# Scaling the halves of the up product ahead of the silu, exchanging two carried products, reordering a leftover pair and pinning row additions in a two-layer trunk

## The chip, the cores and the metric

The kernel runs on one core of one Trainium2 chip. The metric is the device time of one execution in microseconds; the smaller the better. The kernel before took 1260.61 us, the median of 3 runs (1259.55 to 1261.18).

## What is computed

The reference is a trunk of two layers of a hybrid decoder: a residual mixer (attention heads beside retention heads) and a residual SwiGLU feed-forward network (FFN), on 16 learned tokens and 512 given ones, with 1024 features. The change touches the FFN alone:

```python
D_MODEL = 1024; SEQ = 512; DEPTH = 2; N_META = 16
D_FF = -(-8 * D_MODEL // (3 * 256)) * 256        # 2816
...
    mix = jnp.concatenate([fox_out, ret_out], axis=-1)
    h = h + jnp.einsum('blc,cd->bld', mix, w_out)

    hn = rmsnorm(h, ffn_norm_g)
    ff = jax.nn.silu(jnp.einsum('bld,df->blf', hn, w_gate)) * jnp.einsum('bld,df->blf', hn, w_up)
    return h + jnp.einsum('blf,fd->bld', ff, w_down)
...
    h = rmsnorm(h, final_norm)
    return h[:, N_META:]
```

## The kernel before

**Data.** The state h lies transposed in SBUF, eight tiles of 128 features by 528 tokens. Layer 0 works on all 528 columns, the FFN of layer 1 on the 512 that are returned. Each fp32 factor is split into a high part hi, a rounded copy that ScalarE (ACT) makes by a cast, and a low part lo, the rest, that VectorE (DVE) subtracts. A product is the three matmuls hi·xh, hi·xl, lo·xh on TensorE (PE), for each block of 128 of the contraction.

**The FFN in units.** The 2816 hidden features are 22 blocks of 128 (`NF`). Blocks 0 to 2 are done plainly, blocks 3 to 21 by the class `Unit`, one object for each block. A unit computes gate and up of its block together by seven products instead of eight, on half columns (w = 264 in layer 0, 256 in layer 1) and half of the contraction (`HB` = 4 blocks, so 12 matmuls each); `p(i)` gives product i, in the order 1, 2, 6, 5, 7, 4, 3. Products 1, 6, 7 and 4 accumulate into the bank x (pool psa, four buffers of one bank), 2 goes into z, 5 and 3 into y (pool psd, two buffers of two banks). After products 1, 6 and 7 `keep` (L960) copies the bank x on ACT into e (L965), and product 4 then ends x. After product 3, `done` (L971) makes the activation: sg = zy + e (L975), times RSC·R (L977, R is the row's normalisation), silu on ACT (L978, which is the helper's line L407; behind the last block's silu a helper loads the next table of ACT, L409), u = sg·(−RSC)·R (L980), the first half of u times x (L982), the second times e[2] (L983); then u is split into ab and xh (L142 the cast, L143 the subtraction), for every second block after sums of parts (L992, L999 to L1001).

**The FFN's second matrix in pairs.** The hidden blocks are worked off in rounds of four (`ROUNDS`). After a round, the class `Down` multiplies it into h, two output blocks (a pair, p = 0 to 3) at a time, again by seven products, of two blocks (6 matmuls) each. Products 1, 6, 7, 4 go into a psa bank x, 2 into z, 5 and 3 into y of a psd buffer. `keep` (L1078) copies x, and y after product 5, on ACT into S (L1084); so product 4, which adds to x, waits for the copy after product 7, and product 3, which adds to y, for the copy after product 5. `done` (L1099), after product 3, adds z and y to S on DVE (L1102) and so releases the psd buffer. `add` (L1091) adds S to the two rows of h: by an accumulating DMA on POOL's queue, or, for the leftover pair, on DVE (L1097).

**Order.** The lists in the planning loop (L1177 to L1232) interleave the pairs of one round with the units of the next. PE runs in the order of these lists (L1512); the instructions of the other engines are put into an order by a scheduler, unless `pin` (L307) keeps one in the order of the program. Four pairs meet four units, but in the last round only three (blocks 19, 20, 21): the fourth pair, the leftover pair e, follows beside block 21 (L1203). For p = 0 the list (L1191) ends with (d, 7); the two products that are left, 4 and 3, the hang, are carried into the next unit, behind its product 1 (L1201, L1205). Eight such hangs are in the program, four in each layer.

**The last round** (blocks 19 to 21) goes into h plainly: `down_job` (L1115) loads and splits its weights by `splits` (L885: the cast L886, the subtraction L887), `down` (L1132) multiplies (L1148) and adds to h (L1163). In layer 1 the products of this round are planned apart (L1240 on): eight products of the first 272 columns, with row sums on DVE from psa (`add_part`, L1249), then eight of the other 240, among them the final normalisation and the output.

Weights of units: `make1` to `make4`, by `splits` or by ACT (L938) and DVE (L939, L940); weights of pairs: `make_a`, `make_b` (L1058 to L1065), with sums that POOL makes ahead of them (L1050 to L1056).

Of the kernel before, what the change touches and what calls it, by code (L numbers as in the profile page):

```python
# [10 lines left out]
F32 = mybir.dt.float32  # L11
F32R = mybir.dt.float32r
AF = mybir.ActivationFunctionType
ALU = mybir.AluOpType
# [11 lines left out]
NF = DFF // 128  # L26
# [13 lines left out]
def hybrid_kernel(ctx, tc, x_t, w_in, w_fl, w_out, w_gate, w_up, w_down, vecs, b_fg, rope, decay, mask, ident, out_t):  # L40
    nc = tc.nc
# [9 lines left out]
    h = [state.tile([128, T], F32, name=f"h{k}") for k in range(NK)]  # L51
# [89 lines left out]
    def split(hi, lo, src, pinned=False):  # L141
        pin(nc.scalar.copy(hi, src), pinned)  # L142
        pin(nc.vector.tensor_sub(lo, src, hi.bitcast(F32)), pinned)  # L143
# [122 lines left out]
    def tt(name, dt=F32):  # L266
        tag, bufs = tags[name]
        return tmp.tile([128, T], dt, name=name, tag=tag, bufs=bufs)
# [4 lines left out]
    def fft(tag, dt=F32R, shape=(128, T), bufs=None):  # L273
        return phase["ffn"].tile(list(shape), dt, name=tag, tag=tag, bufs=bufs)
# [28 lines left out]
    RSC = -1.0 / (2.0 * D)  # L303
# [3 lines left out]
    def pin(f, pinned=True):  # L307
        if pinned:
            tc.keep_in_program_order(f)
# [96 lines left out]
    def silu(t, then=None):  # L406
        nc.scalar.activation(t, t, AF.Silu)  # L407
        if then:
            tc.keep_in_program_order(nc.scalar.preload_act_table_set(then))  # L409
# [384 lines left out]
    def ffn(l, st, real, last):  # L794
        QC = REAL if real else FULL
        t0 = META if real else 0
        w = (T - t0) // 2
# [5 lines left out]
        def two(t):  # L803
            return t[:, t0:T].rearrange("p (a b) -> p a b", a=2)
# [6 lines left out]
        def act_tile(f):  # L811
            t = buf(0).rearrange("p i s c -> p (i s c)")
            i = f if f < PLAIN else f - ROUNDS[-1][0]
            return [t[:, (2 * i + j) * T:(2 * i + j + 1) * T] for j in range(2)]
# [60 lines left out]
        def add_job(**job):  # L875
            job["ring"] = "f" if len(jobs) % 2 else ""
            jobs.append(job)
            return len(jobs) - 1
# [3 lines left out]
                if i <= j or "make" in jobs[i]:  # L882
                    convert(i)

        def splits(hi, lo, src):  # L885
            nc.scalar.copy(hi, src)  # L886
            nc.vector.tensor_sub(lo, src, hi.bitcast(F32))  # L887

        def product(j, o, x, bank, fresh, final, n=HB, done=None):

# [14 lines left out]
        class Unit:  # L905
# [65 lines left out]
            def done(self):  # L971
                e = self.t["e"]
                sg = tt("sg")
                with tc.high_priority():
                    nc.vector.tensor_add(two(sg), self.t["zy"][:, :, 0:w], e[:, 0:2])  # L975
                c = slice(t0, T)
                nc.vector.scalar_tensor_tensor(sg[:, c], sg[:, c], RSC, st["R"][:, c], ALU.mult, ALU.mult)  # L977
                silu(sg[:, c], None if self.f < NF - 1 else ROOTS if last else LOGS)  # L978
                u = tt("tq")
                nc.vector.scalar_tensor_tensor(u[:, c], sg[:, c], -RSC, st["R"][:, c], ALU.mult, ALU.mult)  # L980
                u2 = two(u)
                nc.vector.tensor_mul(u2[:, 0], self.t["x"][:, 0:w], u2[:, 0])  # L982
                nc.vector.tensor_mul(u2[:, 1], e[:, 2], u2[:, 1])  # L983
                if self.f >= ROUNDS[-1][0]:
                    fh, fl = act_tile(self.f)
                    split(fh[:, c], fl[:, c], u[:, c])
                    acts[self.f] = (fh, fl)
                    return
                q, second = divmod(self.f - PLAIN, 2)
                if not second:  # L990
                    us[q] = u2, two(tt("tq"))
                    nc.vector.tensor_sub(us[q][1][:, 0], u2[:, 1], u2[:, 0])  # L992
                    return
                u0, ta = us.pop(q)
                tb = two(tt("tq"))
                parts = [(0, 1, u0[:, 0:1]), (1, 2, u2), (3, 2, ta), (5, 2, tb)]
                for i, (s, n, src) in enumerate(parts):
                    if i == 2:
                        nc.vector.tensor_sub(tb[:, 0], u2[:, 1], ta[:, 0])  # L999
                        nc.vector.tensor_sub(tb[:, 1], u2[:, 1], u0[:, 1])  # L1000
                        nc.vector.tensor_sub(ta[:, 1], u2[:, 0], tb[:, 0])  # L1001
                    ph, pl = slots(q, s, n, 0), slots(q, s, n, 1)
                    m = n // len(ph)
                    for j in range(len(ph)):
                        split(ph[j], pl[j], src[:, j * m:(j + 1) * m])
# [27 lines left out]
        class Down:  # L1033
# [57 lines left out]
            def add(self, s):  # L1091
                m = 2 * self.m + s
                e = self.t["e"][:, 2 * s:2 * s + 2]
                if self.dma:
                    adds.append(lambda: nc.gpsimd.dma_start(two(h[m]), e, accum_op=ALU.add))  # L1095
                else:
                    nc.vector.tensor_add(two(h[m]), e, two(h[m]))  # L1097

            def done(self):  # L1099
                e = self.t["e"][:, 0:2]  # L1100
# [14 lines left out]
        def down_job(p, f0, f1, own=False):  # L1115

            n = f1 - f0
            t = {}

            def load():  # L1120
                if t:
                    return
                if own:
                    t["r"] = fft("fraw", F32, (128, NK, 128), 2)
                else:
                    t["r"] = wp.tile([128, NK, 128], F32, name="raw", tag="raw", bufs=3)
                for s in range(2):
                    nc.sync.dma_start(t["r"][:, s * n:s * n + n], w_down[l, 2 * p + s, :, f0:f1])

            return add_job(load=load, make=lambda hi, lo: splits(hi, lo, t["r"][:, 0:2 * n]), n=2 * n)  # L1130

        def down(j, s, m, f0, f1, banks, far=False):  # L1132

# [42 lines left out]
        hang = []  # L1176
        for r, (f0, f1) in enumerate(ROUNDS):  # L1177
            for f in range(f0, f1):
                if f < PLAIN:
                    steps += dense_steps(w_gate[l, f], [(0, xs, NK, QC, g_done(f) if f else held.append)], banks=f == 1)  # L1180
                    steps += dense_steps(w_up[l, f], [(0, xs, NK, QC, u_done(f))])
                    continue
                u = Unit(f, r > 1)
                if r > 1 and fills:
                    p = fills.pop(0)[0]
                    if p == 0:
                        u.rest()
                        d = Down(p, r - 1, True)
                        u.last()
                        d.second()  # L1190
                        order = ((u, 1), (u, 2), (u, 6), (u, 5), (u, 7), (d, 1), (d, 2), (u, 4), (d, 6), (d, 5), (u, 3), (d, 7))  # L1191
                    else:
                        d = Down(p, r - 1, True)
                        u.rest()
                        d.second()
                        if f == NF - 1:
                            e = Down(fills.pop(0)[0], r - 1, False)
                        u.last()
                        if f == NF - 1:
                            e.second()  # L1200
                        order = [(u, 1)] + hang + [(u, 2), (d, 1), (u, 6), (d, 2), (u, 5), (d, 6), (u, 7), (d, 5), (d, 7),  # L1201
                                                   (u, 4), (d, 4), (d, 3), (u, 3)]
                        if f == NF - 1:  # L1203
                            order[-1:] = [(e, 1), (u, 3)] + [(e, i) for i in (2, 6, 5, 7, 3, 4)]
                    hang = [(d, 4), (d, 3)] if p == 0 else []  # L1205
                    for o, i in order:
                        steps += o.p(i)
                        if o is u and i == 6 or o is not u and f == NF - 1 and i == 4:
                            steps.append(flush)
                    continue  # L1210
                steps += u.head()
                for v in tails:
                    v.last()
                    steps += v.tail()
                tails = []
                u.rest()
                steps += u.middle()
                if fills:
                    p, g0, g1 = fills.pop(0)
                    j = down_job(p, g0, g1)  # L1220
                    steps += down(j, 0, 2 * p, g0, g1, not real, r < len(ROUNDS) - 1)
                    u.last()
                    steps += u.tail()
                    steps += down(j, 1, 2 * p + 1, g0, g1, False, r < len(ROUNDS) - 1)
                else:
                    tails = [u]
            for p, g0, g1 in fills:
                j = down_job(p, g0, g1)
                for s in range(2):
                    steps += down(j, s, 2 * p + s, g0, g1, False)  # L1230
            assert not fills or r < 2
            fills = [(p, f0, f1) for p in range(NK // 2)]  # L1232
        n = f1 - f0
# [355 lines left out]
```

## Time and profile before

| | |
|---|---|
| median of 3 runs | 1260.61 us (1259.55 to 1261.18) |
| the profiled execution | 1260.84 us, its span 1259.1 us |
| granted TensorE clock, mean | 0.998 |
| PE busy | 1239.7 us (98%), 9463 matmuls |
| weight loads (PEld) busy | 1194.2 us (95%) |
| DVE busy | 1036.9 us (82%), 1980 instructions |
| ACT busy | 782.9 us (62%), 1572 instructions |
| POOL busy | 558.8 us (44%) |

The profile is of one execution, with times from the start of the span. A row of the timeline has the start, the duration, the engine, the line, the operation, the tile that is written and those that are read, their shapes, and in brackets how long the engine was idle just before and what released it. Two instructions of an engine overlap at their ends, so what one costs its engine is read from start to start. A row of the waits says which instruction waited for which, with the sum, the number of times and the longest. A row of the grouped instructions has the count, the busy time in us and the mean in ns. The row of a window has the stretch and its length, then busy us (and instructions) of PE, PEld, DVE, ACT and POOL, the granted clock, the DMA engines' share and GB/s.

### The profile page before, as it was taken

Reading aid. Unit: us, or ns where it says so; the run is one execution under the profiler, and the core shown is the slowest. Engines: PE = TensorE matmul, PEld = TensorE weight load, DVE = VectorE, ACT = ScalarE, POOL = GpSimd, SP = SyncE. Lnnn points to the kernel's source line nnn. Section 1 sums busy time; section 2 is a strip of 40 time slices with the busy share of each in tenths; the row PEclk is TensorE's granted clock in tenths of the full one; section 3 lists DMA queues with packets and bytes.
Section 4 is the critical chain, followed back from the end, with each engine's and each line's share of the span. In section 5 each row is a group of like instructions: output and inputs, shape, how many; then the busy total and the mean of one; then the engine's idle time right before and its main releaser. Section 6 shows DMA issues by size and latency. Waiting matters only on the chain. (4 is left out here: it accounts for less than half of the span.)

```text
span 1259.1 us, 25291 instructions
## 1 busy us (share of the span) xinstructions
PE 1239.7 (98%) x9463; PEld 1194.2 (95%) x9463; DVE 1036.9 (82%) x1980; ACT 782.9 (62%) x1572; POOL 558.8 (44%) x866
## 2 busy tenths in 40 slices
PE   9999999999999999999999999999999999999996
PEld 8999999999999999999999989999789999999996
DVE  7877855779778999899886877567897899999987
ACT  6666545676556666666666665557765566666665
POOL 3355546421135555554325545454112545655440
PEclk9999999999999999999999999999999999999999
DMA  6322232226687878786423222222367877878751
GB/s 219 94 69 85 77 87 82 62 83 181 157 193 160 205 168 209 171 200 148 123 78 119 69 97 80 79 91 68 127 159 187 196 184 186 186 183 189 173 135 67
DMA packets 73051, 170.80 MB, mean 136 GB/s; under 512 B 8400, under 2 KB 15312, under 8 KB 72928
## 3 DMA queue, kind: packets, MB, share of 16 engines
q1 hardware_dynamic: 50576, 128.70, 31.7%
q0 software_dynamic: 21888, 40.17, 19.9%
q8 instruction: 74, 1.21, 0.4%
q14 instruction: 49, 0.40, 0.1%
q10 hardware_dynamic: 464, 0.32, 0.1%
HBM read 146.79 MB, written 2.13 MB: 118 GB/s over the span
## 5 line engine op out<-in xcount | busy, mean ns | idle before, releaser
L194 POOL TENSOR_TENSOR wlo<-raw,whi 128x128 fp32r<-128x128 f32 x504 | 258.6, 548 | 280.4 <-ACT whi L191 280.3
L217 PE MATMUL psd<-xh,whi 128*128 128x264 f32 (+1 forms) x792 | 196.3, 315 | 0.5 <-ACT whi L191 0.5
L217 PE MATMUL psd<-xh,wlo 128*128 128x264 f32 (+1 forms) x792 | 187.0, 304 | 0.0
L217 PE MATMUL psd<-xl,whi 128*128 128x264 f32 (+1 forms) x792 | 186.6, 303 | 0.4 <-DVE xl L320 0.4
L217 PEld LDWEIGHTS psd<-xh,whi 128*128 128x128 f32 x792 | 128.8, 190 | 5.5 <-ACT whi L191 1.2
L217 PEld LDWEIGHTS psd<-xh,wlo 128*128 128x128 f32 x792 | 127.4, 189 | 6.3 <-DVE wlo L194 0.4
L217 PEld LDWEIGHTS psd<-xl,whi 128*128 128x128 f32 x792 | 128.0, 189 | 4.7 <-DVE xl L320 0.8
L191 ACT CAST whi<-raw 128x512 fp32r<-128x512 f32 (+1 forms) x168 | 98.5, 613 | 51.9 <-PE psd L217 36.9
L926 POOL DMA_DIRECT2D Sw<-w_up x38 | 34.0, 911 | 168.1 <-DMA Sw<-w_up 38.0
L1095 POOL DMA_DIRECT2D h<-S x60 | 54.3, 914 | 84.4 <-ACT S L1084 33.1
L887 DVE TENSOR_TENSOR wlo<-raw,whi 128x1024 fp32r<-128x1024 f32 (+1 forms) x62 | 76.7, 1248 | 16.5 <-ACT whi L886 16.3
L886 ACT CAST whi<-raw 128x1024 fp32r<-128x1024 f32 (+1 forms) x62 | 58.8, 954 | 40.4 <-issue 10.3
L898 PE MATMUL psa<-th,fwhi 128*128 128x264 f32 (+1 forms) x256 | 72.5, 283 | 0.0
L898 PE MATMUL psa<-tl,fwhi 128*128 128x264 f32 (+1 forms) x256 | 72.5, 283 | 0.0
L898 PE MATMUL psa<-th,fwlo 128*128 128x264 f32 (+1 forms) x256 | 72.4, 283 | 0.0
L927 POOL DMA_DIRECT2D fraw<-w_gate x38 | 33.4, 880 | 85.4 <-DVE xl L320 40.4
L965 ACT COPY e<-psa 128x264 f32<-128x264 f32 (+1 forms) x114 | 42.6, 374 | 37.3 <-PE psa L898 37.0
L527 ACT ACTIVATE probs<-probs,nmax 128x144 f32<-128x144 f32 (+1 forms) x64 | 36.9, 576 | 44.4 <-DVE nmax L514 31.5
L898 PE MATMUL psa<-ab,fwhi 128*128 128x264 f32 (+3 forms) x304 | 59.7, 285 | 0.7 <-ACT S L1084 0.6
L898 PE MATMUL psa<-th,whi 128*128 128x264 f32 (+1 forms) x200 | 56.8, 284 | 0.2
L898 PE MATMUL psa<-th,wlo 128*128 128x264 f32 (+1 forms) x200 | 56.1, 281 | 0.0
L898 PE MATMUL psa<-tl,whi 128*128 128x264 f32 (+1 forms) x200 | 56.1, 281 | 0.0
(370 smaller groups left out, 4468.5 us busy)
## 6 DMA issues: line engine op xcount, KB each, us to landing
raw<-w_in SPq DMA_DIRECT2D x54, 512.0 KB, 3.5
raw<-w_gate SPq DMA_DIRECT2D x44, 512.0 KB, 4.9
fraw<-w_up SPq DMA_DIRECT2D x38, 512.0 KB, 5.8
raw<-w_down SPq DMA_DIRECT2D x64, 256.0 KB, 4.3
h<-S POOLq DMA_DIRECT2D x38, 264.0 KB, 5.3
Sw<-w_up SPq DMA_DIRECT2D x38, 256.0 KB, 3.9
fraw<-w_gate POOLq DMA_DIRECT2D x38, 256.0 KB, 4.1
Sw<-w_up POOLq DMA_DIRECT2D x38, 256.0 KB, 6.6
```

Source lines behind the costliest of these rows:

```text
L191: pin(nc.scalar.copy(hi, job["raw"][:, c0:c1]), pinned)
L194: pin(sub(lo[:, i:i + step], job["raw"][:, c0 + i:c0 + i + step], hi[:, i:i + step].bitcast(F32)), pinned)
L217: nc.tensor.matmul(ps[1][b][:, 0:c1 - c0], w[:, wk, :], x[:, c0:c1], start=(k == 0 and i == 0), stop=(k == n - 1 and i == 2))
L527: nc.scalar.activation(pr, pr, AF.Exp, bias=nmax[0:nq], scale=-1.0, accum_out=rsum)
L886: nc.scalar.copy(hi, src)
L887: nc.vector.tensor_sub(lo, src, hi.bitcast(F32))
L898: nc.tensor.matmul(bank()[:, 0:b.shape[-1]], a[:, o + k, :], b, start=(fresh and k == 0 and i == 0), stop=(k == n - 1 and i == 2), skip_gr ...
L926: nc.gpsimd.dma_start(s, w_up[l, self.f][:, 0:HB], accum_op=ALU.add)
L927: nc.gpsimd.dma_start(self.t["b"][:, 0:HB], w_gate[l, self.f][:, 0:HB], accum_op=ALU.add)
L965: nc.scalar.copy(self.t["e"][:, i], self.t["x"][:, 0:w])
L1095: adds.append(lambda: nc.gpsimd.dma_start(two(h[m]), e, accum_op=ALU.add))
```

## The change

Five edits:

1. `splits` gets an argument `pinned`; the subtraction of the last round's weights, for the pairs p = 2 and 3, is kept in program order.
2. In `Unit.done`, x and e[2] are scaled by −RSC·R into the two halves of u ahead of the silu (two scalar_tensor_tensor of a half each). Behind the silu stands one product u = sg·u over all columns, in place of a whole scalar_tensor_tensor and two products of a half.
3. In `Down.add`, the addition of rows on DVE (the leftover pair alone) is kept in program order.
4. The leftover pair's products go in the order 1, 5, 6, 2, 7, 3, 4 instead of 1, 2, 6, 5, 7, 3, 4.
5. The hang is product 3, then 4, instead of 4, then 3. Each is followed by its own row addition, so the two accumulating DMAs are issued in the other order too.

```diff
-        def splits(hi, lo, src):
+        def splits(hi, lo, src, pinned=False):
             nc.scalar.copy(hi, src)
-            nc.vector.tensor_sub(lo, src, hi.bitcast(F32))
+            pin(nc.vector.tensor_sub(lo, src, hi.bitcast(F32)), pinned)
...
                 nc.vector.scalar_tensor_tensor(sg[:, c], sg[:, c], RSC, st["R"][:, c], ALU.mult, ALU.mult)
+                u = tt("tq")
+                u2, r2 = two(u), two(st["R"])
+                for i, v in enumerate((self.t["x"][:, 0:w], e[:, 2])):
+                    nc.vector.scalar_tensor_tensor(u2[:, i], v, -RSC, r2[:, i], ALU.mult, ALU.mult)
                 silu(sg[:, c], None if self.f < NF - 1 else ROOTS if last else LOGS)
-                u = tt("tq")
-                nc.vector.scalar_tensor_tensor(u[:, c], sg[:, c], -RSC, st["R"][:, c], ALU.mult, ALU.mult)
-                u2 = two(u)
-                nc.vector.tensor_mul(u2[:, 0], self.t["x"][:, 0:w], u2[:, 0])
-                nc.vector.tensor_mul(u2[:, 1], e[:, 2], u2[:, 1])
+                nc.vector.tensor_mul(u[:, c], sg[:, c], u[:, c])
...
-                    nc.vector.tensor_add(two(h[m]), e, two(h[m]))
+                    pin(nc.vector.tensor_add(two(h[m]), e, two(h[m])))
...
-            return add_job(load=load, make=lambda hi, lo: splits(hi, lo, t["r"][:, 0:2 * n]), n=2 * n)
+            return add_job(load=load, make=lambda hi, lo: splits(hi, lo, t["r"][:, 0:2 * n], f1 == NF and p > 1), n=2 * n)
...
-                            order[-1:] = [(e, 1), (u, 3)] + [(e, i) for i in (2, 6, 5, 7, 3, 4)]
-                    hang = [(d, 4), (d, 3)] if p == 0 else []
+                            order[-1:] = [(e, 1), (u, 3)] + [(e, i) for i in (5, 6, 2, 7, 3, 4)]
+                    hang = [(d, 3), (d, 4)] if p == 0 else []
```

In the changed kernel the scaled halves are line 981 and the product is line 983.

The scheduler makes another order of it on ACT and DVE too. On PE, the third hang of layer 0, a piece of the difference; psd is the buffer of product 3, psa with xh of 4144 that of product 4, ab the operand slots of the round:

```order
 L898 MATMUL psa<-xl_4153,whi 128x264
 L898 MATMUL psa<-xh_4152,wlo 128x264
+L898 MATMUL psd<-ab_4348,fwhi 128x264 x2
+L898 MATMUL psd<-ab_4348,fwlo 128x264
+L898 MATMUL psd<-ab_4346,fwhi 128x264 x2
+L898 MATMUL psd<-ab_4346,fwlo 128x264
 L898 MATMUL psa<-xh_4144,fwhi 128x264
 L898 MATMUL psa<-xl_4145,fwhi 128x264
```

Product 3 stands directly behind the unit's product 1 (its last rows are the two without a sign); product 4 follows.

On ACT, the end of the leftover pair and of block 21 in layer 1, before (S is the pair's sum tile, sg and tq belong to block 21's activation, fwhi and fraw to the last round's weights):

```order
L1084 COPY S<-psa 128x256
L886 CAST fwhi<-fraw 128x768
L1084 COPY S<-psd 128x256
L1084 COPY S<-psa 128x256
L407 ACTIVATE sg<-sg 128x512
L409 ACT_TABLE_LOAD
L1084 COPY S<-psa 128x256
L886 CAST fwhi<-raw 128x768
L142 CAST ab_12249<-tq 128x512
```

The same place after:

```order
L1084 COPY S<-psd 128x256
L1084 COPY S<-psa 128x256
L407 ACTIVATE sg<-sg 128x512
L886 CAST fwhi<-fraw 128x768
L1084 COPY S<-psa 128x256
L409 ACT_TABLE_LOAD
L1084 COPY S<-psa 128x256
L142 CAST ab_12249<-tq 128x512
L886 CAST fwhi<-raw 128x768
```

The copy of psd (product 5) and the silu moved ahead of the cast of fraw, and the cast of ab ahead of that of raw.

On DVE, the same stretch, before:

```order
L975 TENSOR_TENSOR sg<-psd,e 128x512
L887 TENSOR_TENSOR wlo<-fraw,whi 128x768
L977 SCALAR_TENSOR_TENSOR sg<-sg,R 128x512
L887 TENSOR_TENSOR fwlo<-fraw,fwhi 128x768
L1086 TENSOR_TENSOR S<-S 128x256
L1102 TENSOR_TENSOR S<-psd,S 128x512
L980 SCALAR_TENSOR_TENSOR tq<-sg,R 128x512
L1097 TENSOR_TENSOR h_79<-S,h_79 128x512
L982 TENSOR_TENSOR tq<-psa,tq 128x256
L983 TENSOR_TENSOR tq<-e,tq 128x256
L1097 TENSOR_TENSOR h_80<-S,h_80 128x512
L887 TENSOR_TENSOR fwlo<-raw,fwhi 128x768
```

After, up to the first row sum of the last round:

```order
L977 SCALAR_TENSOR_TENSOR sg<-sg,R 128x512
L983 TENSOR_TENSOR tq<-sg,tq 128x512
L887 TENSOR_TENSOR fwlo<-fraw,fwhi 128x768
L1102 TENSOR_TENSOR S<-psd,S 128x512
L1086 TENSOR_TENSOR S<-S 128x256
L1097 TENSOR_TENSOR h_79<-S,h_79 128x512
L143 TENSOR_TENSOR ab_12249<-tq,ab_12249 128x512
L887 TENSOR_TENSOR wlo<-fraw,whi 128x768
L1097 TENSOR_TENSOR h_80<-S,h_80 128x512
L887 TENSOR_TENSOR fwlo<-raw,fwhi 128x768
L1249 TENSOR_TENSOR h_73<-psa,h_73 128x272
L1249 TENSOR_TENSOR h_74<-psa,h_74 128x272
```

The scaled halves stand further ahead, outside these rows; L977 follows L975 directly, and the subtraction wlo<-fraw, which stood between them, comes behind L143. Before, L143 stood behind the last row shown, and L1249 behind it.

## The prediction

> **What bounds the kernel now.** I read the page first, then the waits of TensorE and of its weight loads, then those stretches of the timeline in which the longest of the waits lie.
>
> ```profile
> span 1259.1 us, 25291 instructions
> PE 1239.7 (98%) x9463; PEld 1194.2 (95%) x9463; DVE 1036.9 (82%) x1980; ACT 782.9 (62%) x1572; POOL 558.8 (44%) x866
> ```
>
> TensorE (PE) is busy for 98% of the span, and the change adds and removes no matmul. So at most the time in which PE stands still can be won, and only at places that the change touches. I take the waits from the weight loads (PEld), since a product begins with one. Columns: time in all, times, longest.
>
> ```profile
> PEld psa L898 <- ACT S L1084: 2.2, 4, 0.6
> PEld psa L898 <- DVE ab L143: 1.9, 4, 1.2
> PEld psd L1148 <- DVE ab L143: 1.1, 1, 1.1
> PEld psd L898 <- ACT S L1084: 1.1, 2, 0.6
> PEld psd L898 <- DVE ab L143: 0.9, 4, 0.3
> PEld psa L898 <- ACT e L965: 0.8, 3, 0.3
> PEld psa L898 <- ACT ab L142: 0.6, 1, 0.6
> ```
>
> These seven rows are the FFN's stalls in and around the pairs: 8.6 us in 19 waits. Each is a product that waits for the copy of its bank (L1084, L965), or for the cast or the subtraction of an operand (L142, L143). What one costs is read from the starts of PE's matmuls; the first two rows are of the second hang of layer 0, the next two of the leftover pair of layer 1, the last two of that layer's final round.
>
> ```profile
> 459.35 0.28 PE L898 MATMUL psa<-xl,whi 128*128 128x264 f32 x1
> 459.46 0.28 PE L898 MATMUL psa<-xh,wlo 128*128 128x264 f32 x1
> 459.99 0.51 PE L898 MATMUL psa<-ab,fwhi 128*128 128x264 f32 x2 [0.25 <-ACT S L1084]
> ...
> 1226.07 0.28 PE L898 MATMUL psa<-xh,fwlo 128*128 128x256 f32 x1
> 1226.69 0.51 PE L898 MATMUL psd<-ab,fwhi 128*128 128x256 f32 x2 [0.34 <-ACT S L1084]
> ...
> 1230.97 0.39 PE L898 MATMUL psa<-ab,whi 128*128 128x272 f32 x1 [0.34 <-ACT ab L142]
> 1232.39 0.39 PE L898 MATMUL psa<-ab,whi 128*128 128x272 f32 x1 [1.03 <-DVE ab L143]
> ```
>
> An unbroken step from start to start is 0.11 to 0.12 (459.35 to 459.46), so the six matmuls of a product of two blocks take about 0.7. The steps into the stalls are 0.53 and 0.62: they cost 0.41 and 0.50, where the weight loads list up to 0.6. I take 0.05 off each wait of the seven rows.
>
> **The exchanged hang.** Why product 4 waits at 459.99 is on ACT:
>
> ```profile
> 458.00 0.62 ACT L886 CAST fwhi<-sqh 128x512 fp32r<-128x512 f32 x1 [1.06 <-POOL sqh L1054]
> ...
> 459.06 0.62 ACT L938 ACTIVATE whi<-Sw 128x512 fp32r<-128x512 f32 x1
> 459.58 0.36 ACT L1084 COPY S<-psa 128x264 f32<-128x264 f32 x1
> ```
>
> The copy of product 7's bank stands behind weight casts and ends at 459.94; PE goes on 0.05 later. With product 3 first, PE has six matmuls on another bank (psd, whose copy was long done): 0.7 of cover for stalls of at most 0.6. Four of the eight hangs stall (first row of the waits), so the gain is 2.2 − 4 × 0.05 = **2.0**. Product 3 now ends 0.7 earlier, so L1102 may run earlier; product 4 ends 0.7 later, and behind it are only a copy, a row addition by an accumulating DMA, and the release of its psa bank, one of four. With them the two accumulations exchange their places on POOL's queue; the transfer behind them there (Sw, L926) is for weights that a later unit takes. I cost both at nothing; if that cover were gone, a product would wait as long as those of this row, 0.5.
>
> **The order of the leftover pair.** Product 3 of it waits at 1226.69 for the copy of product 5's bank, which stands behind a weight cast:
>
> ```profile
> 1224.94 0.37 ACT L1084 COPY S<-psa 128x256 f32<-128x256 f32 x1 [0.67 <-PE psa L898]
> 1225.53 0.83 ACT L886 CAST fwhi<-fraw 128x768 fp32r<-128x768 f32 x1 [0.22 <-PE psd L898]
> 1226.27 0.36 ACT L1084 COPY S<-psd 128x256 f32<-128x256 f32 x1
> 1226.80 0.64 ACT L407 ACTIVATE sg<-sg 128x512 f32<-128x512 f32 x1
> 1227.46 1.28 ACT L409 ACT_TABLE_LOAD   x1
> 1228.75 0.37 ACT L1084 COPY S<-psa 128x256 f32<-128x256 f32 x1
> 1230.30 0.62 ACT L142 CAST ab<-tq 128x512 fp32r<-128x512 f32 x1 [0.44 <-DVE tq L983]
> ```
>
> Moved to the front, product 5 ends three products (2.2 us) ahead of product 3, and its copy stands ahead of the cast: 1.1 − 2 × 0.05 = 1.0 goes. What is late next is product 4, for the copy of product 7's bank. In layer 1 that copy is put behind silu (1225.21) and cast (0.54 and 0.74 later) and ends at about 1226.87, while PE wants the bank at 1226.91, with 0.05 to 0.1 of signalling: under 0.1 in one layer, by the same walk 0.13 in the other. Term: **0.8**.
>
> **Halves ahead of the silu, in the last block.** In block 21, what matters is when the split of its activation ends (L143), since the layer's last round waits for it (1.1 in layer 0, 0.6 and 1.2 in layer 1).
>
> ```profile
> 1224.30 0.96 DVE L887 TENSOR_TENSOR wlo<-fraw,whi 128x768 fp32r<-128x768 f32 x1
> 1225.18 0.68 DVE L977 SCALAR_TENSOR_TENSOR sg<-sg,R 128x512 f32<-128x512 f32 x1
> 1226.40 0.96 DVE L887 TENSOR_TENSOR fwlo<-fraw,fwhi 128x768 fp32r<-128x768 f32 x1 [0.53 <-ACT fwhi L886]
> ...
> 1228.31 0.69 DVE L980 SCALAR_TENSOR_TENSOR tq<-sg,R 128x512 f32<-128x512 f32 x1
> ...
> 1229.85 0.42 DVE L983 TENSOR_TENSOR tq<-e,tq 128x256 f32<-128x256 f32 x1
> 1230.18 0.69 DVE L1097 TENSOR_TENSOR h<-S,h 128x512 f32<-128x512 f32 x1
> 1230.78 0.95 DVE L887 TENSOR_TENSOR fwlo<-raw,fwhi 128x768 fp32r<-128x768 f32 x1
> 1231.65 0.69 DVE L143 TENSOR_TENSOR ab<-tq,ab 128x512 fp32r<-128x512 f32 x1
> ```
>
> On DVE a 512-wide operation takes 0.60 from start to start, a 256-wide 0.33, a 768-wide 0.88. Before, silu begins at 1226.80, two DVE rows and four small ones follow, and the split ends at 1232.34. After, by the order of both engines: L977 stands directly behind L975, silu starts at 1225.21 behind the copy of 1224.94 and ends at 1225.85, the one product sg·u ends at 1226.58; ACT does the cast and copy to 1226.9, the table load to 1228.18, a copy (0.27), and the cast of ab to 1229.08; L143 starts 0.05 later and ends at 1229.82. PE wants it at 1230.34 + 0.12 − 0.4 (half of the last term) = 1230.06. So 0.6 + 1.2 − 2 × 0.05 = 1.7 goes here. In layer 0 the same rows move by the same 2.5 us, and 1.1 is needed: 1.05 goes.
>
> What is late next: DVE's pinned rows now stand between L143 and the first row sum L1249. From L143's start, 0.60 + 0.88 (wlo) + 0.60 (L1097) + 0.88 (fwlo) puts L1249 at 1232.09, and it releases its bank at about 1232.52. The fifth product of the last round needs that bank 18 matmuls after 1230.06, at 0.125 each 1232.31, and sees it 0.05 to 0.1 after its release: a new stall of 0.3. Term: 1.7 + 1.05 − 0.3 = **2.4** (2.7 if the stall doesn't come).
>
> **The same in the other blocks.** Before, u is complete one 528-wide and two 264-wide steps after silu, after, one 528-wide step:
>
> ```profile
> L980 DVE SCALAR_TENSOR_TENSOR tq<-sg,R 128x528 f32<-128x528 f32 x19 | 13.3, 699 | 0.0
> L982 DVE TENSOR_TENSOR tq<-psa,tq 128x264 f32<-128x264 f32 x19 | 8.1, 424 | 0.1
> L983 DVE TENSOR_TENSOR tq<-e,tq 128x264 f32<-128x264 f32 x19 | 8.0, 421 | 0.0
> ```
>
> That is 0.67 sooner. The waits after a pair's second unit (1.9 − 1.2, 0.9, and 0.8: 2.4 in 10 waits of at most 0.3 each) are shorter than that: 2.4 − 10 × 0.05 = 1.9. The copy L965 still has one cast of a part ahead of it in layer 1, which leaves 0.6 by the walk of ACT's order. Term: **1.3** (0.7 if twice as much stays, 1.9 if nothing does).
>
> The operation count on DVE stays: 528 + 264 + 264 becomes 264 + 264 + 528. The new form, a scaled product of 264 from PSUM, isn't in the trace: it lies between 0.42 (L982, same bank and width) and 0.70 (L980, same operation, twice as wide). I take 0.42. What is costed at nothing is that 0.67 of DVE work now stands ahead of the silu, and ahead of L1102, which releases a psd buffer that the next unit's second product wants:
>
> ```profile
> 1055.88 0.69 DVE L1102 TENSOR_TENSOR S<-psd,S 128x512 f32<-128x512 f32 x1
> ...
> 1057.09 0.28 PE L898 MATMUL psd<-xh,whi 128*128 128x256 f32 x1
> ```
>
> L1102 ends at 1056.57, 0.52 ahead of the matmul. A round of layer 1, busy us of PE, PEld, DVE and the others:
>
> ```profile
> 1064.00:1125.00 61.00, 60.40 (x505) 59.53 (x504) 57.17 (x96) 39.11 (x79) 35.89 (x41) 1.00 0.80 190
> ```
>
> DVE is idle for 3.8 us of 61, a good part of it in waits for casts just ahead of L1102, where the moved halves can go. I take that as cover. If it failed, 0.1 to 0.2 per unit.
>
> **Sum.** 2.0 + 0.8 + 2.4 + 1.3 = 6.5. The profiled execution took 1260.84 (its span and 1.74 around it), 0.23 above the median 1260.61; 6.5 off the median gives **1254.1**. What a measurement here can tell from no change is 0.2%, 2.5 us: the forecast is well beyond it.
>
> **Rivals.** *Part is given back* (0.18): the halves ahead of silu make releases late where cover is thin. At 0.1 for each of the 32 releases by L1102, 3.2 come back: 1257.3. For it: 0.52 of slack against 0.67 of moved work. Against it: DVE's gaps.
>
> *A table load that costs more* (0.04). The trace shows 1.28 us, and ACT's next copy starts 0.01 after its end (1227.46 + 1.28 = 1228.74, 1228.75). The chain to the split now leads through that load. If as much again stood behind it, the split of layer 1, 0.24 early by the walk, would be 1.0 late, and that of layer 0 (2.5 − 1.0, less the 0.9 that PE comes sooner, so 0.6 early) 0.7: 1.7 come back, 1255.8. The Trainium skill (ScalarE: Activation LUTs, What ACT_TABLE_LOAD costs) puts a drain of about 1380 ns behind the load of about 1283 ns; by that the two would be 0.1 later still, an estimate from that page of 1256.0. The trace agrees on the load and shows no drain behind it.
>
> *Waits only move* (0.08): the next operand on the same engines is late by what was won; 1260, within 0.2%. For it: DVE at 94% in that round. Against it: I walked what is next, and what I found (0.2, 0.3 and 0.6) is in the sum already.
>
> *Slower* (0.05): the PSUM halves cost like whole ones, 0.6 per half. Then 1.2 of work stands ahead of L1102 against a slack of 0.52: each of 32 releases is late by 0.7, or by 0.4 where an idle stretch takes 0.3: 32 × 0.4 = 12.8, less the 6.5, gives 1266.9. It decides above (6.5 + 2.5) / 32 = 0.28 per release. Against it: L982 reads the same bank in 0.424, L983 reads none in 0.421.
>
> The forecast has 0.65. The range goes from the sum without any new stall (6.5 + 0.2 + 0.3 + 0.6: 1253.0) to the first rival (1257.3), at either end with the 1.1 by which the fastest of the runs before, 1259.55, lies from their median: 1251.9 to 1258.4. The forecast's 0.65, the table load's 0.04 and 0.15 of the first rival's 0.18 are beyond 2.5: faster 0.84; its rest and the moved waits are within: 0.11; slower 0.05.
>
> **What would show it.** Right: in the waits of the weight loads after the change the rows of psa and psd on ACT S L1084 shrink from 3.3 to under 0.5, the one of psd L1148 is gone, and PE's starts in the hangs go on at 0.12. The row of silu in block 21 of layer 1 stands near 1225.2 less what was won before, and its table load directly ahead of a copy. A new row psa L898 on DVE h L1249 of 0.3 is the stall that I add. Wrong: rows psd L898 on DVE S L1102, the price of the first rival and, if long, of the last; L981 from psa above 0.45; or waits of the same sum under other names.

## The result and the profile after

The changed kernel took 1253.38 us, the median of 5 runs (1252.6 to 1255.0), the kernel before 1260.11 in the same series (1259.55 to 1261.18). The ratio is 0.9946, with a 95% interval of 0.9934 to 0.9957: 6.8 us less (5.4 to 8.3). Forecast were 1254.1 and a gain of 6.5.

The page of the changed kernel, its span and its busy times:

```profile
span 1251.3 us, 25269 instructions
PE 1235.4 (99%) x9463; PEld 1192.8 (95%) x9463; DVE 1038.6 (83%) x1980; ACT 781.8 (62%) x1572; POOL 556.9 (45%) x866
```

As many matmuls as before, in a span that is 7.8 shorter. Not all of this is the change. The start of one matmul early in layer 0's attention and of the first of the last sums tells how much (before, then after):

```profile
40.64 0.39 PE L507 MATMUL psa<-kh,qs 128*128 128x272 f32 x1 [0.80 <-DVE nmax L514]
...
1248.86 0.38 PE L1320 MATMUL psa<-sqh,ones 128*128 128x240 f32 x1 [1.25 <-ACT sqh L1370]
```

```profile
39.78 0.40 PE L507 MATMUL psa<-kh,qs 128*128 128x272 f32 x1 [0.53 <-DVE nmax L514]
...
1241.07 0.38 PE L1320 MATMUL psa<-sqh,ones 128*128 128x240 f32 x1 [1.25 <-ACT sqh L1370]
```

Ahead of the first, where nothing was changed, 0.86 differs from one profile to the other; between the two, 1208.22 became 1201.29, so 6.93 are left. A second profile of the changed kernel (the last experiment) starts 1.7 later at that place and has 1201.64 between the two. That is why the experiments below are read by the median ratio and by the rows of the waits, not by one span.

The waits of the weight loads after the change, the rows of the FFN:

```profile
PEld psa L898 <- ACT e L965: 2.4, 5, 0.8
...
PEld psa L898 <- DVE h L1249: 0.3, 1, 0.3
...
PEld psd L1148 <- DVE h L1163: 0.3, 1, 0.3
```

Of the seven rows quoted in the prediction, 8.6 in 19 waits, six are gone: all on S L1084, on ab L143 and on ab L142. A small one that the prediction left out, psa L898 on wlo L887 (0.2), is gone too. The seventh, the copy L965, grew from 0.8 in 3 to 2.4 in 5. The row on h L1249 is the new stall that the prediction had added; the one on h L1163 stood there before (0.3). The sum of the seven and the new one is 2.7, so 5.9 less.

The end of layer 1 on ACT, the stretch shown of before; everything is 5.8 us earlier there:

```profile
1219.14 0.37 ACT L1084 COPY S<-psa 128x256 f32<-128x256 f32 x1 [0.34 <-PE psa L898]
1219.41 0.64 ACT L407 ACTIVATE sg<-sg 128x512 f32<-128x512 f32 x1
...
1221.06 1.28 ACT L409 ACT_TABLE_LOAD   x1
1222.35 0.37 ACT L1084 COPY S<-psa 128x256 f32<-128x256 f32 x1
1222.62 0.62 ACT L142 CAST ab<-tq 128x512 fp32r<-128x512 f32 x1
```

From the copy behind product 6 (1219.14) the forecast had the silu 0.27 later, the table load's end 3.24 later, the cast's 4.14, and the end of the split on DVE 4.88. Measured: 0.27, 3.20, 4.10 and, below, 4.83. The table load ends at 1222.34 and the next copy begins at 1222.35: nothing stands behind the load, on the path too.

On DVE and PE the same:

```profile
1223.28 0.69 DVE L143 TENSOR_TENSOR ab<-tq,ab 128x512 fp32r<-128x512 f32 x1
...
1226.23 1.48 DVE L1249 TENSOR_TENSOR h<-psa,h 128x272 f32<-128x272 f32 x4
```

```profile
1224.18 0.42 PE L898 MATMUL psa<-ab,whi 128*128 128x272 f32 x2
...
1226.32 0.29 PE L898 MATMUL psa<-ab,fwlo 128*128 128x272 f32 x1
1226.71 0.40 PE L898 MATMUL psa<-ab,whi 128*128 128x272 f32 x1
```

The split L143 ends at 1223.97, and PE takes the operand at 1224.18 without a wait. The row sum L1249 begins behind the three rows that stand ahead of it (left out here: L887, L1097, L887), and the fifth product starts at 1226.71, 0.39 after its neighbour in place of 0.125: the stall of 0.3.

### The profile page after: what moved, and what is told of

Its sections match the earlier page's. It is cut to its first block, busy times and chain, and to the rows that moved or that the text cites. A ratio compares the mean times of both kernels' runs of the same rounds, so it can differ in the third digit from the quotient of the medians.

```text
span 1251.3 us, 25269 instructions
## 1 busy us (share of the span) xinstructions
PE 1235.4 (99%) x9463; PEld 1192.8 (95%) x9463; DVE 1038.6 (83%) x1980; ACT 781.8 (62%) x1572; POOL 556.9 (45%) x866
## 5 line engine op out<-in xcount | busy, mean ns | idle before, releaser
L887 DVE TENSOR_TENSOR wlo<-raw,whi 128x1024 fp32r<-128x1024 f32 (+1 forms) x62 | 70.1, 1131 | 20.9 <-ACT whi L886 20.8
L898 PE MATMUL psa<-th,fwhi 128*128 128x264 f32 (+1 forms) x256 | 72.5, 283 | 0.0
L898 PE MATMUL psa<-tl,fwhi 128*128 128x264 f32 (+1 forms) x256 | 72.5, 283 | 0.0
L898 PE MATMUL psa<-th,fwlo 128*128 128x264 f32 (+1 forms) x256 | 72.4, 283 | 0.0
L965 ACT COPY e<-psa 128x264 f32<-128x264 f32 (+1 forms) x114 | 42.5, 373 | 38.6 <-PE psa L898 38.5
L898 PE MATMUL psa<-ab,fwhi 128*128 128x264 f32 (+3 forms) x304 | 58.8, 283 | 0.0
L898 PE MATMUL psa<-th,whi 128*128 128x264 f32 (+1 forms) x200 | 56.7, 284 | 1.4 <-ACT e L965 1.1
L407 ACT ACTIVATE sg<-sg 128x528 f32<-128x528 f32 (+1 forms) x48 | 30.6, 638 | 43.0 <-DVE sg L977 40.5
L898 PE MATMUL psa<-tl,whi 128*128 128x264 f32 (+1 forms) x200 | 56.2, 281 | 0.0
```

Source lines behind the costliest of these rows:

```text
L898: nc.tensor.matmul(bank()[:, 0:b.shape[-1]], a[:, o + k, :], b, start=(fresh and k == 0 and i == 0), stop=(k == n - 1 and i == 2), skip_gr ...
L965: nc.scalar.copy(self.t["e"][:, i], self.t["x"][:, 0:w])
```

## The experiments

Twelve kernels, in three series. The kernel before had medians of 1261.12, 1260.9 and 1260.5 beside them, so ratios to it are compared. An edit also lets the scheduler put the instructions of ACT and DVE into another order, so a run shows the worth of an edit together with the order that it brings.

**The hang alone.**

```diff
-                    hang = [(d, 4), (d, 3)] if p == 0 else []
+                    hang = [(d, 3), (d, 4)] if p == 0 else []
```

> The kernel before with the exchanged hang alone. Theory (every stall of the hang goes and nothing takes its place; in the trace each of the four cost about 0.5 and 0.1 more at the matmul behind it): 2.4 us faster than before, about 1257.7, and no row psa L898 on ACT S L1084 among the waits of the weight loads. Rival (the wait only moves, to the copy that the next product needs): the time of before, 1260.1, and a row of about 2 us under another name in the stretch behind the hangs.

Measured: ratio 0.9975 (0.9965 to 0.9985), 3.2 us less (1.9 to 4.4). The row psa on S L1084 is gone. The one of the leftover pair (psd) stays, and so do those at the layers' ends, 1.1 and 1.2:

```profile
PEld psa L898 <- DVE ab L143: 1.7, 3, 1.2
...
PEld psd L898 <- ACT S L1084: 1.1, 2, 0.6
```

The theory holds: product 3 covers the copy. But not all of the 3.2 is that row: the waits on ab L143 and on the copy L965 behind the pairs shrank too, from 2.4 in 10 to 1.1 in 5, and the row on wlo L887 grew from 0.2 to 0.6. The order of POOL's transfers is the one of before; in particular the two row additions of a hang did not change places.

**The leftover pair's order alone.**

```diff
-                            order[-1:] = [(e, 1), (u, 3)] + [(e, i) for i in (2, 6, 5, 7, 3, 4)]
+                            order[-1:] = [(e, 1), (u, 3)] + [(e, i) for i in (5, 6, 2, 7, 3, 4)]
```

> The kernel before with the new order of the leftover pair alone. Theory A (at a layer's end one chain counts, the end of block 21's split, L143; what PE wins at the pair it waits again unless the split comes sooner too; by the order L143 now stands ahead of a 768-wide subtraction, 0.9 sooner): 1.8 to 2.0 us faster, about 1258.2, with the row psd L898 on ACT S L1084 gone and the waits on ab L143 at the layers' ends shorter by about 0.3 each only. Theory B (edits add up, each stall for itself): 1.2 us faster, 1258.9, with the waits on ab L143 at the ends as before. Rival C (moved altogether): 1260.1, the waits on ab L143 longer by 0.6 each.

Measured: ratio 0.9985 (0.9976 to 0.9994), 1.9 us less (0.8 to 3.0).

```profile
PEld psa L898 <- ACT S L1084: 3.0, 6, 0.6
PEld psa L898 <- DVE ab L143: 1.6, 4, 1.0
...
PEld psd L1148 <- DVE ab L143: 0.3, 1, 0.3
```

The interval holds theories A and B; the rows speak for A. PE comes to the last round sooner, and yet its waits there fell: 1.1 to 0.3 in layer 0, 0.6 and 1.2 to 1.0 in layer 1. So the split comes sooner through this edit too. Two new waits came into the row on S L1084: product 4 of the leftover pair, for the copy of product 7's bank, which the prediction had priced for the whole change (0.2) and which is larger here, with the late silu.

**The halves alone, nothing pinned.** Of the diff only the part in `Unit.done`.

> The kernel before with the halves of up scaled ahead of the silu alone, nothing pinned. Theory A (one chain at each layer's end): the split of block 21 comes about 1.2 sooner, enough for layer 0, not for layer 1, where some 0.7 of waiting on ab stays; the first products behind a pair win 0.5 in all; about 3.0 us faster, 1257.1, with the four stalls of the hang and the two of the leftover pair as before. Theory B (edits add up): all of the gain at the ends belongs to this edit, 3.3 us, 1256.8, and no wait on ab at either end. Rival (the halves ahead of the silu cost releases): a row psd L898 on DVE S L1102 and less than 1.5 us won, above 1258.6.

Measured: ratio 0.9972 (0.9961 to 0.9982), 3.5 us less (2.3 to 4.9).

```profile
PEld psa L898 <- ACT e L965: 2.9, 5, 0.8
...
PEld psa L898 <- DVE ab L143: 1.1, 1, 1.1
PEld psa L898 <- ACT S L1084: 0.9, 3, 0.5
PEld psd L1148 <- DVE ab L143: 0.4, 1, 0.4
...
PEld psd L898 <- DVE S L1102: 0.2, 1, 0.2
```

Waits on ab stay at both ends (0.4 and 1.1), so theory B is out: the halves do not bring the whole gain there. Two things none of the theories had: the hang's stalls shrank (2.2 in 4 to 0.9 in 3), and the copy L965 is waited for longer (0.8 to 2.9). Once a release by L1102 is late, by 0.2.

**All but the halves.** The changed kernel, with the old lines behind the silu.

> The changed kernel with the old form behind the silu (whole product, then two halves), all else as changed. Theory A: hang 2.4, and at the layers' ends the pair's order and the pinned rows bring L143 about 1.3 sooner each, so 2.4 + 2.6 = 5.0 faster than before, 1255.1, with about 0.7 of waiting on ab left in layer 1; the waits on the copy e L965 are as before the change, 0.8 in 3. Theory B (edits add up): the gain of the ends is missing whole, 3.6 faster than before, 1256.5, with the waits on ab at both ends as long as before.

Measured: ratio 0.9964 (0.9951 to 0.9976), 4.5 us less (3.0 to 6.2).

```profile
PEld psa L898 <- DVE ab L143: 1.2, 4, 0.5
PEld psa L898 <- ACT e L965: 0.8, 3, 0.4
PEld psd L1148 <- DVE h L1163: 0.6, 1, 0.6
...
PEld psa L898 <- DVE h L1249: 0.5, 1, 0.5
```

The time decides nothing between A and B. The rows do: no wait on ab is left at the end of layer 0 and 0.5 at the end of layer 1. Not all of it is won, though: in layer 0 the wait on h L1163 grew from 0.3 to 0.6, and in layer 1 there is 0.5 on h L1249. All in all, the waits at the ends fell from 3.2 to 1.6. So about half of them go without the halves. The copy L965 is waited for as long as before the change, so the growth of that row belongs to the halves; by the order of ACT, too, the casts ahead of it are as many as before the change here, and with the halves alone as many as in the changed kernel.

**Nothing pinned.** The changed kernel without its two new pins.

> The changed kernel with nothing newly pinned: by the order, DVE does two 768-wide subtractions and L1102 before the product sg·u at the ends of both layers, and ACT does the silu behind the cast of fraw. Theory (the pins place the split's chain, and the split is what the last round waits for): the wait on h L1249 (0.3) goes and waits on ab L143 of 0.3 to 1.0 at each layer's end come, 0.3 to 1.3 slower than the changed kernel, ratio to before 0.9950 to 0.9958. Rival (the pins are for the rows of h alone and cost 0.3 at L1249): 0.3 faster than the changed kernel, ratio 0.9944, no wait on ab at the ends.

Measured: ratio 0.9938 (0.9925 to 0.9950).

```profile
PEld psa L898 <- ACT S L1084: 0.8, 2, 0.4
```

The theory falls: no wait on ab comes back. As the rival had it, the wait on h L1249 goes; but product 4 of the leftover pair waits instead, 0.4 in each layer, for a copy that stands behind a silu that stands behind a cast. The pins win nothing that these runs can show.

**The old hang, and the old order of the pair, in the changed kernel.** Each of the two diffs above, backwards.

> The changed kernel with the old hang, product 4 ahead of product 3. Theory (the edits overlap: with the halves alone the hang's stalls had shrunk from 2.2 in 4 to 0.9 in 3, so the exchange has less to take away): a row psa L898 on ACT S L1084 of 0.8 to 1.0, about 1.2 slower than the changed kernel. Rival (edits add up): a row of 2.2 in 4, 2.4 to 3 slower than the changed kernel.

> The changed kernel with the old order of the leftover pair (1, 2, 6, 5, 7, 3, 4). Theory (the edits overlap: by the order the copy of product 5's bank stands ahead of the cast of fraw here too, behind a silu that begins 1.6 sooner than before): no row psd L898 on ACT S L1084 above 0.2, within 0.3 of the changed kernel. Rival (edits add up): the row of 1.1 in 2 is back, 1.2 slower than the changed kernel.

Measured: 0.9955 (0.9943 to 0.9968) and 0.9950 (0.9936 to 0.9963), where the changed kernel itself had 0.9947 (0.9935 to 0.9960) in the same series. The old hang, then the old order:

```profile
PEld psa L898 <- ACT S L1084: 0.5, 2, 0.3
```

```profile
PEld psa L898 <- ACT S L1084: 0.5, 2, 0.2
```

The first is the hang's row, the second product 4 of the leftover pair; neither row of before is back in its size (psa 2.2 in 4, psd 1.1 in 2). The hang's row is smaller even than expected (0.8 to 1.0). The edits overlap: with the halves ahead of the silu, ACT's order is another, and the copies come sooner by themselves. Alone the three edits gave 3.2, 1.9 and 3.5, in sum 8.6; together they gave 7.8 with nothing pinned (6.3 to 9.5) and 6.8 with the pins. The times alone do not show an overlap. The waits do: of the 9.1 that are listed for the FFN's weight loads before (the seven rows, 0.3 on h L1163 and 0.2 on wlo L887) the hang alone takes 3.1, the pair's order 2.2 and the halves 2.2, in sum 7.4; the three together, nothing pinned, 5.7.

**The copy ahead of the casts.** The changed kernel; the late casts are issued after the copy and kept in that order:

```diff
+        late = []
...
-                        nc.scalar.copy(self.t["e"][:, i], self.t["x"][:, 0:w])
+                        pin(nc.scalar.copy(self.t["e"][:, i], self.t["x"][:, 0:w]), i == 2 and late)
...
+                    if i == 2:
+                        for _, (hi, lo, src) in sorted(late, key=lambda v: v[0]):
+                            pin(nc.scalar.copy(hi, src))
+                            nc.vector.tensor_sub(lo, src, hi.bitcast(F32))
+                        late.clear()
...
-                        split(ph[j], pl[j], src[:, j * m:(j + 1) * m])
+                        one = (ph[j], pl[j], src[:, j * m:(j + 1) * m])
+                        if i > 1 and self.f + 1 in [r[0] for r in ROUNDS[2:]]:
+                            late.append(((5, 3, 6, 4).index(s + j), one))
+                        else:
+                            split(*one)
...
-                splits(hi, lo, r[:, 2:NK])
+                pin(nc.scalar.copy(hi, r[:, 2:NK]), self.m == 0)
+                nc.vector.tensor_sub(lo, r[:, 2:NK], hi.bitcast(F32))
...
+                        jobs[u.w3]["far"] = False
```

> The changed kernel with the casts of a round's last two parts (operands 3 to 6) put behind the copy L965 of the next unit's product 7 on ACT, instead of ahead of it; the cast of the first pair's second weights is put behind them. Theory (the five waits of product 4 on that copy, 2.2 us and 0.1 more behind each, come from casts that stand ahead of the copy in ACT's queue and wait for DVE, though the bank has long been ready): the row on e L965 goes from 2.4 in 5 to under 0.5, 2.0 to 2.7 faster than the changed kernel, ratio to before 0.9925 to 0.9930. Rival (the bank is ready late, or the casts put back make the operands late): the waits stay, or move to ab L142 and L143 in the products 6 and 5 behind; ratio 0.9942 to 0.9955.

Measured: ratio 0.9946 (0.9933 to 0.9960), as the changed kernel. In this kernel's lines L1096 is the copy L1084, and L974 a subtraction that was put back.

```profile
PEld psa L898 <- ACT S L1096: 1.7, 2, 0.9
PEld psa L898 <- DVE ab L974: 1.6, 3, 0.7
```

Half of the theory is shown: with the casts behind the copy, no wait on it is left. The other half falls: 3.3 of waits came back under other names, at the subtractions that were put back and at product 4 of two hangs.

A second form did this only at two boundaries of each layer and kept the subtractions ahead of a scaled half.

> As the kernel with the casts of operands 3 to 6 put behind the copy L965, but only at the two boundaries of each layer where these operands lie in the shared buffers, and there with the subtractions of these operands ahead of the next unit's scaled half on DVE. Theory (the earlier form lost what it won at two places, the hang behind the last boundary, 0.8 each, and the subtractions behind a scaled half, 0.3 to 0.6 each): the row on e L965 falls from 2.4 in 5 to 0.6 to 1.0 in 2, a rest of 0.3 on ab; 1.0 to 1.6 faster than the changed kernel. Rival (what is put back is late whatever stands ahead): as fast as the changed kernel or slower, with waits on ab or S of over 1.0 in all.

Measured: ratio 0.9958 (0.9946 to 0.9971). L1097 is the copy L1084.

```profile
PEld psa L898 <- ACT S L1097: 2.4, 3, 1.1
```

The copy L965 is still waited for at the two boundaries that were left as they were, 0.9 in all. The waits on ab are gone, those of product 4 in the hang came. The rival is right both times. Neither form beats the changed kernel.

**The price of work ahead of the silu.** One half, and both halves, scaled twice.

```diff
-                for i, v in enumerate((self.t["x"][:, 0:w], e[:, 2])):
+                for i, v in ((0, self.t["x"][:, 0:w]), (0, self.t["x"][:, 0:w]), (1, e[:, 2])):
```

```diff
-                for i, v in enumerate((self.t["x"][:, 0:w], e[:, 2])):
+                for i, v in 2 * ((0, self.t["x"][:, 0:w]), (1, e[:, 2])):
```

> The changed kernel in which the half of up that is read from psa is scaled twice, one behind the other, in every unit from block 3 on (the second writes the same values again): 38 operations of 0.34 more on DVE ahead of the silu. Theory (the moved work lies in DVE's idle stretches ahead of L1102 and has cover): under 1.5 us slower than the changed kernel, ratio to before 0.9946 to 0.9958. Rival (no cover, each adds its time to the release of the psd buffer): up to 38 times 0.34, 13 us slower, ratio above 1.000, with rows psd L898 on DVE S L1102.

> The changed kernel in which both halves of up are scaled twice (the second writes the same values again): 38 times 0.34 and 0.34 to 0.6 more on DVE ahead of the silu, 0.7 to 0.9 per unit where a round of four units had 3.8 us idle before. Theory (cover that runs out): 3 to 10 us slower than the changed kernel, ratio 0.997 to 1.003, with waits on DVE's operations in the FFN under several names, S L1102 among them. Rival A (still covered): ratio under 0.996. Rival B (no cover from the start): 30 us slower, ratio about 1.02.

Measured: 0.9980 (0.9971 to 0.9989) and 1.0048 (1.0035 to 1.0061), against 0.9946 for the changed kernel 4.3 and 12.9 us more. One half twice, then both:

```profile
PEld psa L898 <- ACT e L965: 6.5, 8, 1.6
...
PEld psd L898 <- DVE S L1102: 0.3, 1, 0.3
```

```profile
PEld psa L898 <- ACT e L965: 7.4, 8, 1.6
PEld psa L898 <- ACT S L1084: 3.9, 6, 1.0
PEld psd L898 <- DVE S L1102: 3.5, 6, 0.9
```

Both theories on the first miss: 0.34 more in each of 38 units is neither covered (under 1.5) nor paid whole (13), but a third of it. And it is not paid where the prediction looked: the psd releases still have cover. What is waited for is the copy L965. In six of the eight places it stands directly behind casts of parts of u, which come late. At the third boundary of layer 1, where ACT's order up to the copy is that of the changed kernel, the wait grew from 0.76 to 1.17, about the 0.34 that was added. But part of the price is the scheduler's: the longest wait, 1.6, at layer 1's first boundary, is behind a cast of weights (fwhi<-raw) that waits for L1064, which now stands later on DVE; in the changed kernel there is no wait at that place. Only the second step makes the releases late too, and the kernel slower than before. Its theory named the right waits, but 12.9 is more than the 3 to 10 that it gave.

**The changed kernel again.**

> The changed kernel itself, for the comparison within one chip. Expected 6.8 below the kernel before, ratio 0.9946, with the row on e L965 of 2.4 in 5.

Measured: ratio 0.9947 (0.9935 to 0.9960), with 2.5 in 5 on e L965.

## Why the prediction was right, and where it was not

*What bounds the kernel* was right: PE's work stayed, and the gain is that of its stalls. *The size of a stall* was a little low. I took 0.05 off each wait of the weight loads. (Of the starts of PE that I showed for it, three rows are of the hang, not two.) The matmul behind a stalled one comes late too, as at the third boundary of layer 1 in the changed kernel:

```profile
1118.70 0.40 PE L898 MATMUL psa<-ab,fwhi 128*128 128x256 f32 x2
...
1120.02 0.28 PE L898 MATMUL psd<-ab,fwlo 128*128 128x256 f32 x1
1120.85 0.39 PE L898 MATMUL psa<-th,whi 128*128 128x256 f32 x1 [0.56 <-ACT e L965]
1121.08 0.28 PE L898 MATMUL psa<-tl,whi 128*128 128x256 f32 x1
1121.19 0.28 PE L898 MATMUL psa<-th,wlo 128*128 128x256 f32 x1
```

The step behind the stall is 0.23, the next 0.11. With that 0.1, a wait costs what the weight loads list or somewhat more, not less.

*The hang* (2.0) was right in its mechanism: alone, its row is gone and 1.9 to 4.4 are won. What it says of POOL is not so, nor is the same remark ahead of it: by the order, the two row additions of a hang keep their places in the changed kernel. What changes, at three hangs of layer 1, is that the transfer Sw goes behind the second of them, and that comes with the halves. No wait came of it. *The pair's order* (0.8) and *the last block* (2.4) were right for the whole change: none of their waits is left but the 0.3 at L1249 that was added. But I gave the whole of the last block's term to the halves. The runs show that it has several owners. Of the 3.2 of waits at the two ends before (ab L142 and L143, h L1163) the pair's order alone leaves 1.6, all but the halves 1.6 (with h L1249), the halves alone 1.8, and the whole change 0.6. The chain itself shows it best: from the start of the copy behind product 6 to the end of the split L143 in layer 1 it takes 7.40 before, 6.73 with the halves alone, 6.46 with the pair's order alone, 5.56 with all but the halves, and 4.83 with everything. So the halves are worth 0.7 of the 2.5 that the prediction put down to them. A term was tied to an edit, where it belongs to a chain that several edits shorten.

*The same in the other blocks* (1.3) is the step that failed. It held that u comes 0.67 sooner and the waits behind a pair shrink by as much. The waits on ab L143 did go (1.6 in 7), but those on the copy L965 grew by 1.6, so next to nothing was won by the rows. The halves do both: with them alone no such wait on ab is left and the copy's row is 2.9. On ACT, the same boundary before, then after:

```profile
1124.74 0.61 ACT L142 CAST ab<-tq 128x512 fp32r<-128x512 f32 x1
1125.26 0.36 ACT L965 COPY e<-psa 128x256 f32<-128x256 f32 x1
1125.53 0.62 ACT L142 CAST ab<-tq 128x512 fp32r<-128x512 f32 x1
```

```profile
1119.39 1.14 ACT L142 CAST ab<-tq 128x512 fp32r<-128x512 f32 x2 [1.25 <-DVE tq L1000]
1120.43 0.37 ACT L965 COPY e<-psa 128x256 f32<-128x256 f32 x1
```

Product 7 of the unit, whose bank is copied, stood ahead of the pair's twelve matmuls that run from 1118.70 to 1120.02, so the copy could have run in the 1.25 in which ACT waited for DVE. It stood behind two casts of parts, where before one of them came behind it, and product 4, due 0.12 after 1120.02, started at 1120.85. The prediction had one cast of a part ahead of the copy at that place, as before. That the casts ahead of it make the wait is shown by the kernel that puts them behind it; that moving them wins time is not.

*The rivals.* Part given back did not come at its place: a psd release was late once, by 0.2, in two of the kernels with the new halves (leaving out the two that scale a half twice), and none in the changed one. The table load cost what it showed. That waits only move is right for the failed term, and for my two attempts to mend it. The slower rival did not come: a half from psa took 0.42, not 0.6. Its price, 1266.9, lies near what both halves scaled twice gave (1.0048 of the kernel before, 1266.2 from its 1260.11), but that says nothing for its mechanism: more work was added there, and only 3.5 of the waits are at the releases that the rival named.

That the sum came out within 0.3 of the measured gain is partly luck, because errors cancel: 1.3 too much for the other blocks; 0.2 too little for the pair, whose added wait did not come, and about 0.1 too little on each of the nine stalls of the hang, the pair and the ends. With these put right it would be 6.3. The waits as listed account for the measured 6.8: they fell from 9.1 in 21 to 3.0 in 7, so 6.1, and each of the 14 that are gone had cost some 0.05 more than listed.

## What to carry to other kernels

List the stalls of the engine that bounds, and for each what stands ahead of its releaser in that engine's queue; a copy that was ready long ago behind a cast that waits costs as much as a late copy. Before giving a gain to an edit, ask which edits shorten the same chain: here three of them took 7.4 of waits one by one, and 5.7 together. Idle time on an engine is no proof that added work is free: 0.34 more in each unit cost 4.3, and it was paid not at the releases that the prediction watched but at copies that stand behind casts on another engine.

## What the runs showed of the hardware

The half of up that lies in SBUF often costs more than the one in PSUM. The 19 units of layer 0 in the changed kernel:

```profile
L981 DVE SCALAR_TENSOR_TENSOR tq<-e,R 128x264 f32<-128x264 f32 x19 | 11.6, 611 | 0.5
...
L981 DVE SCALAR_TENSOR_TENSOR tq<-psa,R 128x264 f32<-128x264 f32 x19 | 8.0, 423 | 8.7 <-PE psa L898 8.7
```

I had taken 0.42 for both, by the row of L983 before (421 ns), which has two SBUF operands as well. One place, DVE and then POOL:

```profile
1063.44 0.68 DVE L981 SCALAR_TENSOR_TENSOR tq<-e,R 128x256 f32<-128x256 f32 x1
1064.04 0.41 DVE L981 SCALAR_TENSOR_TENSOR tq<-psa,R 128x256 f32<-128x256 f32 x1
```

```profile
1062.66 1.17 POOL L1054 TENSOR_TENSOR sqh<-sqh,raw 128x128 f32<-128x128 f32 x1
1063.80 2.11 POOL L1056 TENSOR_TENSOR raw<-raw 128x128 f32<-128x128 f32 x2
```

Both halves run beside POOL's sums of weights; the one that reads SBUF twice takes 0.68, the one that reads PSUM 0.41. Over both layers, the half from SBUF took 0.42 to 0.44 at the 10 places of 38 where none of these sums runs beside it; at the other 28 it took over 0.6 in 19 (1.74 in one) and 0.42 to 0.50 in nine, so not every such meeting costs. The half from PSUM took 0.41 to 0.43 at all 38. In the new place, ahead of the silu, the half often meets these sums; in the old one the second half (L983) met them at three of 38, and took 0.41 to 0.42 there too. The Trainium skill (SBUF — State Buffer, Who interferes with whom) says that a DVE instruction with two SBUF inputs contends with a GpSimd instruction that reads SBUF, and one with a single SBUF input, outside certain modes, doesn't. The trace agrees with that: 0.68 against 0.41. In layer 0 it cost DVE 19 × 0.19, 3.6 us, of which 1.3 are the one of 1.74.
